# Sums of weight blocks on GpSimd in place of VectorE, in a fused encoder layer

## The chip, the cores and the metric

The kernel runs on one core of a Trainium2 chip. The metric is the device time of one execution in microseconds, taken as the median of several runs. A profile of one execution gives the rows that are read below. In it PE is the matrix engine TensorE (PEld its weight loads), DVE is VectorE, ACT is ScalarE, POOL is GpSimd and SP is SyncE, which issues most DMA transfers.

## What is computed

One layer of an encoder on 256 tokens of width 2048, in float32. After an attention half with two groups of heads comes a feed-forward half, and the change lies in that one:

```python
def conv_ffn(h, w_up_l, conv_w_l, conv_b_l, w_down_l):
    u = h @ w_up_l                       # 2048 -> 2 x 5632
    u = causal_depthwise_conv(u, width=3) + conv_b_l
    gate, val = jnp.split(u, 2, axis=-1)
    return (jax.nn.silu(gate) * val) @ w_down_l    # 5632 -> 2048

x = x + hybrid_mixer(rms_norm(x), ...)
x = x + conv_ffn(rms_norm(x), w_up, conv_w, conv_b, w_down)
```

## The kernel before

**Split weights.** Each float32 factor of a matmul is split in two parts, a rounded high part and the rest, and a product takes three matmuls: high by high, high by low and low by high. A block of weights is 128 partitions by 2048 numbers (1 MB). `load` (L201) issues its transfer on SP's queue into one of four raw buffers (`w_raw`). `split` makes the two parts: ScalarE rounds the block into `w_hi` (L208), then VectorE subtracts that from the raw block into `w_lo` (L209). There are three buffers for each part.

**The feed-forward half** is a list of steps. An up piece multiplies half of the depth for two blocks of 128 up-projection columns: 16 wide matmuls with the high part (L714) and 16 half-wide ones with the low part (L719), alternating two by two. After every second piece its result is evicted, on VectorE and ScalarE: L628 and L630 join the two halves of the accumulator and scale by the token factor, L637 and L644 form the convolution's terms, L649 adds them, and L655, L664, L667 and L669 form the gated product and its split.

**Products of blocks.** The hidden width is taken in parts: one of 4 blocks, then five of 8. While the up pieces of one part run, the down projection of the part before is done. For a part of 8 blocks this is `down_in_seven`, twice, for each half of the output columns. It multiplies 2 x 2 blocks of activations by 2 x 2 blocks of weights in seven products rather than eight, which needs sums of weight blocks. `w11`, `w12`, `w21` and `w22` are blocks of weights (1 MB each), and "w" is a buffer `w_sum`, of which there is one:

- product 1 uses "11", product 2 uses "21";
- product 3 uses "w" = "11" + "12" (the first sum);
- product 4 uses "w" = "w" + "22" (the second sum, in place);
- product 5 uses "12" + w22, product 6 uses "22", and product 7 uses "w" + w21. The additions for products 5 and 7 are made by transfers that accumulate into the block while they load it, issued from GpSimd's queue (L760).

There are four such parts, so 16 sums and 16 accumulating transfers. A product is 12 matmuls (L229) into a bank called `bank_a`, `bank_b` or `bank_c`; L733 then adds it to the tokens `x`. Activations need sums of their own (L678 to L691), once in a part.

**The order** of TensorE, VectorE, ScalarE and SP is written out by hand. At each step of the list the loop emits the loads of the step six ahead, the split of the step two ahead, the sums of the step four ahead, the matmuls of the step itself, and pieces of work that follow earlier steps:

```python
LOAD, SUM, SPLIT = 6, 4, 2
...
at(LOAD, 0)
follow()
at(SPLIT, 2)
follow()
at(SUM, 1)
at(0, 3)
```

Within a part, products alternate with up pieces, so that two steps lie between a product and the next. GpSimd is not in the hand-written order: the framework puts its instructions in order, and they wait for what they read and overwrite. All engines run their queues in order.

## Time and profile before

| | before |
|---|---|
| median of 3 runs | 1131.57 us (1130.93 to 1132.05) |
| span of the profiled execution, first to last instruction | 1129.0 us |
| TensorE busy | 1114.8 us, 99% of the span |
| VectorE busy | 843.3 us, 75% |
| ScalarE busy | 680.6 us, 60% |
| GpSimd busy | 20.9 us, 2% |
| HBM | 225.14 MB read, 201 GB/s over the span |

The profiled execution is told by its span; the median of the runs is 2.6 us longer. Rows of groups read: line, engine, operation, output<-input, shapes, count, then busy time in us and mean ns of one, then the idle time of that engine just before, with what ended it. Rows of the timeline read: start, duration, engine, line, operation, and in brackets idle time before it. Consecutive VectorE operations overlap a little in these rows: one of 2.28 us is followed by the next after 2.20. Rows of the chain read: start, length, what.

### The profile page before, as it was taken

The numbers are of one execution on the slowest core, as the hardware profiler recorded it, in microseconds if no ns is written. First come the engines' busy times: TensorE is split into PE (matmuls) and PEld (weight loads), VectorE is DVE, ScalarE is ACT, GpSimd is POOL, SyncE is SP. The second block draws the span as 40 slices with busy tenths as digits, with TensorE's granted clock in tenths as the row PEclk, the third lists the DMA queues.
The fourth block names the chain that finished last, engine by engine and source line by source line (L and its number), as shares of the span: only waits on it lengthen the run. The fifth ranks groups of instructions, "written<-read, shape, count | busy, mean of one in ns | idle before, by whom it ended". The sixth has DMA issues, their size and how long they took to land.

```text
span 1129.0 us, 14661 instructions
## 1 busy us (share of the span) xinstructions
PE 1114.8 (99%) x5890; PEld 956.6 (85%) x5890; DVE 843.3 (75%) x873; ACT 680.6 (60%) x840; POOL 20.9 (2%) x20
## 2 busy tenths in 40 slices
PE   7999999999999999999999999999999999999998
PEld 6998888888888888888888888888888888888886
DVE  4646656646556666766699898989989798989983
ACT  5644444445664566666667667766776667766751
POOL 0000000000000000000000000000000000000000
PEclk9999999999999999999999999999999999999999
DMA  7766555555444486555649697687949797696951
GB/s 234 219 206 218 171 158 159 185 159 178 149 149 150 149 256 199 188 190 192 195 144 252 220 268 249 187 265 195 290 149 242 240 252 242 188 288 182 291 172 66
DMA packets 170989, 228.17 MB, mean 202 GB/s; under 512 B 3992, under 2 KB 117802, under 8 KB 170922
## 3 DMA queue, kind: packets, MB, share of 16 engines
q1 hardware_dynamic: 162474, 210.47, 57.7%
q0 software_dynamic: 8448, 16.78, 8.6%
q8 instruction: 46, 0.75, 0.3%
q14 instruction: 21, 0.17, 0.0%
HBM read 225.14 MB, written 2.10 MB: 201 GB/s over the span
## 4 chain that ended last, share of the span: by engine, by line
PE 97%; DVE 1%; DMA 1%; ACT 0%; issue 0%; SPq 0%; DVEq 0%; ACTq 0%
PE pu L714 29%; PE acc L229 26%; PE pu L719 15%; PE bank_a L229 10%; PE pu L261 5%; PE bank_b L229 4%; PE pu L266 3%; PE bank_c L229 1%; DVE w_lo L209 1%; PE ps_x L148 1%; DMA x<-in_x_dram 0%; DMA w_raw<-in_w_up_dram 0%; PE ps_h L301 0%; ACT w_hi L208 0%; PE ps_z L511 0%
## 5 line engine op out<-in xcount | busy, mean ns | idle before, releaser
L209 DVE TENSOR_TENSOR w_lo<-w_raw,w_hi 128x2048 fp32r<-128x2048 f32 (+2 forms) x204 | 449.6, 2206 | 196.7 <-ACT w_hi L208 193.4
L208 ACT CAST w_hi<-w_raw 128x2048 fp32r<-128x2048 f32 (+2 forms) x204 | 376.0, 1843 | 248.5 <-PE acc L229 79.6
L714 PE MATMUL pu<-hT,w_hi 128*128 128x512 f32 x1408 | 441.7, 395 | 0.0
L719 PEld LDWEIGHTS pu<-hT,w_lo 128*128 128x128 f32 x1408 | 263.8, 188 | 65.8 <-DVE w_lo L209 4.6
L719 PE MATMUL pu<-hT,w_lo 128*128 128x256 f32 x1408 | 277.6, 278 | 0.9 <-DVE w_lo L209 0.9
L714 PEld LDWEIGHTS pu<-hT,w_hi 128*128 128x128 f32 x1408 | 218.8, 189 | 4.7
L229 PE MATMUL acc<-w_hi,hT 128*128 128x512 f32 (+1 forms) x640 | 143.3, 374 | 0.0
L229 PEld LDWEIGHTS acc<-w_hi,hT 128*128 128x128 f32 x640 | 114.2, 190 | 16.8
L261 PE MATMUL pu<-hT,w_hi 128*128 128x512 f32 x256 | 81.4, 399 | 0.0
L644 ACT ACTIVATE tap<-up,ccol 128x256 f32<-128x256 f32 x176 | 74.6, 495 | 0.0
L229 PE MATMUL acc<-w_lo,hT 128*128 128x512 f32 (+1 forms) x320 | 74.3, 371 | 0.0
L229 PEld LDWEIGHTS acc<-w_lo,hT 128*128 128x128 f32 x320 | 57.8, 189 | 8.7
L209 DVE TENSOR_TENSOR w_lo<-w_sum,w_hi 128x2048 fp32r<-128x2048 f32 x24 | 54.9, 2287 | 12.9 <-ACT w_hi L208 12.9
L208 ACT CAST w_hi<-w_sum 128x2048 fp32r<-128x2048 f32 x24 | 45.8, 1909 | 22.4 <-PE pu L714 20.0
L266 PEld LDWEIGHTS pu<-hT,w_lo 128*128 128x128 f32 x256 | 48.1, 188 | 11.4
L266 PE MATMUL pu<-hT,w_lo 128*128 128x256 f32 x256 | 50.4, 278 | 0.0
L229 PE MATMUL bank_a<-w_hi,g 128*128 128x512 f32 x192 | 47.0, 390 | 0.0
L229 PE MATMUL acc<-w_hi,oT 128*128 128x512 f32 x192 | 46.3, 393 | 0.0
L229 PEld LDWEIGHTS acc<-w_hi,oT 128*128 128x128 f32 x192 | 35.4, 188 | 7.0
L229 PEld LDWEIGHTS bank_a<-w_hi,g 128*128 128x128 f32 x192 | 34.5, 188 | 6.1
L261 PEld LDWEIGHTS pu<-hT,w_hi 128*128 128x128 f32 x256 | 39.0, 189 | 0.0
L637 ACT ACTIVATE gate<-up,ccol 128x256 f32<-128x256 f32 x44 | 24.0, 593 | 18.4 <-DVE up L630 18.4
(177 smaller groups left out, 1098.8 us busy)
## 6 DMA issues: line engine op xcount, KB each, us to landing
w_raw<-in_w_up_dram SPq DMA_DIRECT2D x88, 1024.0 KB, 9.9
w_raw<-in_w_down_dram SPq DMA_DIRECT2D x44, 1024.0 KB, 5.2
w_raw<-in_w_in_dram SPq DMA_DIRECT2D x36, 1024.0 KB, 5.3
w_raw<-in_w_out_dram SPq DMA_DIRECT2D x16, 1024.0 KB, 5.3
w_raw<-in_w_in_dram SPq DMA_DIRECT2D x12, 688.0 KB, 4.9
w_raw<-in_w_down_dram POOLq DMA_DIRECT2D x8, 1024.0 KB, 12.4
w_sum<-in_w_down_dram POOLq DMA_DIRECT2D x8, 1024.0 KB, 9.0
w_raw<-in_w_in_dram SPq DMA_DIRECT2D x8, 512.0 KB, 6.3
```

The source lines that it names most:

```text
L148: nc.tensor.transpose(ps[:, j, t * P : (t + 1) * P], xt[t][:, (k + j) * P : (k + j + 1) * P], ident)
L208: act.copy(hi[:, :n], raw[:, :n])
L209: dve.tensor_tensor(lo[:, :n], raw[:, :n], f32(hi[:, :n]), op=ALU.subtract)
L229: nc.tensor.matmul(o, lhs(i, l, t), r[:, i, :], start=starts and j == 0, stop=stops and j == 3 * n - 1, skip_group_check=len(accs) == 1 an ...
L261: nc.tensor.matmul(acc[:, j, :], hi[:, i, j * P : (j + 1) * P], hT[:, k].rearrange("p a b -> p (a b)"), start=k == 0, stop=False,)
L266: nc.tensor.matmul(acc[:, j, S:], lo[:, i, j * P : (j + 1) * P], hT[:, k, 0, :], start=False, stop=k == KT - 1,)
L637: act.activation(a[:, j, :], u[:, j, 2:], AF.Identity, scale=ccol[:, 2, f : f + 1], bias=ccol[:, 3, f : f + 1],)
L644: act.activation(taps[w][:, j, :], u[:, j, w : w + S], AF.Copy, scale=ccol[:, w, f : f + 1])
L714: nc.tensor.matmul(acc[:, j, :], hi[:, i, j * P : (j + 1) * P], hT[:, k].rearrange("p a b -> p (a b)"), start=k == 0, stop=False,)
L719: nc.tensor.matmul(acc[:, j, S:], lo[:, i, j * P : (j + 1) * P], hT[:, k, 0, :], start=False, stop=k == KT - 1,)
```

## The change

The two sums in each half of a part are issued on GpSimd rather than VectorE. Operands, buffers and shapes stay as they are.

```diff
             def sums():
                 if into not in mem:
                     mem[into] = wsum.tile([P, 2048], F32, name="w_sum", tag="w_sum")
-                dve.tensor_tensor(mem[into], mem[a], mem[b], op=ALU.add)
+                nc.gpsimd.tensor_tensor(mem[into], mem[a], mem[b], op=ALU.add)
 
             return sums
```

In the instruction lists, VectorE has 16 fewer rows, all L781. GpSimd has those 16 and one setup row ahead of them; its order is sum, accumulating transfer, sum, accumulating transfer, and so on. TensorE, ScalarE and SP have the same rows in the same order.

## The prediction

> **What bounds the kernel now.** I read the page first: its span, the busy time of each engine, and the chain that ended last.

> ```profile
> span 1129.0 us, 14661 instructions
> ...
> PE 1114.8 (99%) x5890; PEld 956.6 (85%) x5890; DVE 843.3 (75%) x873; ACT 680.6 (60%) x840; POOL 20.9 (2%) x20
> ...
> PE 97%; DVE 1%; DMA 1%; ACT 0%; issue 0%; SPq 0%; DVEq 0%; ACTq 0%
> ```

> The span is 1129.0 us and TensorE (PE) carries 97% of the chain, so the time is TensorE's own work. VectorE (DVE) is busy 75% of the span, but the sums run only in the FFN stage, so I asked the windows for that stage (columns: length, then busy time and instruction count of PE, weight load, DVE, ACT, POOL).

> ```profile
> 721.00:785.00 64.00, 63.79 (x336) 54.12 (x336) 57.69 (x47) 44.34 (x49) 3.73 (x3) 1.00 0.83 240
> ```

> Here VectorE works 57.69 of 64 us, and still TensorE lacks only 0.21 us. What TensorE lost to VectorE over the four parts that contain sums is in the waits (us in total, times, longest).

> ```profile
> PEld pu L719 <- DVE w_lo L209: 3.9, 8, 0.6
> ...
> PE pu L719 <- DVE w_lo L209: 0.6, 3, 0.2
> ```

> So VectorE is nearly full but almost never late. How much that costs is read from the chain. Each part runs 14 products (2.73 us) with an up piece between each two, and an undisturbed distance from product to product is 779.99 - 771.70 = 8.29 us.

> ```profile
> 712.92 2.73 PE bank_a L229 x12
> ...
> 729.99 2.75 PE bank_b L229 x12
> ...
> 738.52 2.73 PE bank_a L229 x12
> ...
> 771.70 2.73 PE bank_a L229 x12
> ...
> 779.99 2.73 PE bank_c L229 x12
> ...
> 796.58 2.73 PE bank_a L229 x12
> ```

> From the first product at 712.92 to the third at 729.99 it is 17.07 where two distances are 16.58, and to the fourth 8.53: 0.49 + 0.24 = 0.73 us lost in this part. The four parts with sums, which are built alike, lose about 4 x 0.73 = 2.9 us. That is all the change can win by making VectorE lighter. The profiled execution has a span of 1129.0, which is 2.6 below the median of 1131.57; the differences below are worked out inside that execution and laid on the median. About 0.2%, 2.3 us, is what a measurement of this kernel can tell from no change.

> **What moves.** The 16 sums leave VectorE's queue, four to a part.

> ```profile
> L781 DVE TENSOR_TENSOR w_sum<-w_sum,w_raw 128x2048 f32<-128x2048 f32 x8 | 18.3, 2288 | 0.3 <-DMA w_raw<-in_w_down_dram 0.2
> L781 DVE TENSOR_TENSOR w_sum<-w_raw 128x2048 f32<-128x2048 f32 x8 | 18.3, 2283 | 0.0
> ```

> That is 36.6 us of VectorE work, 2.20 each as a place in the queue (720.27 - 718.07 below). Nothing else changes place on VectorE, ScalarE, TensorE or SP. GpSimd's queue gets one setup row ahead of its first sum, which waits for nothing and stands in front of all of them, in a queue that is idle until the FFN stage: nothing; then, for each half of a part: sum, accumulating transfer into block "12", second sum, accumulating transfer into the sum. Both transfers' issues stood behind VectorE before, one after the first sum, the other after the low part of the second sum was split off.

> ```profile
> 720.88 1.28 POOL L760 DMA_DIRECT2D w_raw<-in_w_down_dram  x1 [54.24 <-DVE w_sum L781]
> 737.70 1.28 POOL L760 DMA_DIRECT2D w_sum<-in_w_down_dram  x1 [15.54 <-DVE w_lo L209]
> ```

> Now the first stands behind GpSimd's own sum, and the second sum stands behind the 1.28 us of the first issue. The second transfer (issued at 737.70) still waits for VectorE's split of the second sum and not for its own engine; its block is used only by the seventh product. These moves are free as long as a sum lasts under about 6 us (second rival).

> **How long a sum takes on GpSimd (T).** No row of before shows GpSimd arithmetic. The nearest from below is the same operation on VectorE, 2.28 us. From above there is the other way in which this queue adds one block onto another, the accumulating transfer, 9.0 us to landing.

> ```profile
> w_raw<-in_w_down_dram SPq DMA_DIRECT2D x44, 1024.0 KB, 5.2
> ...
> w_sum<-in_w_down_dram POOLq DMA_DIRECT2D x8, 1024.0 KB, 9.0
> ```

> The middle of the two in ratio is the square root of 2.28 x 9.0, 4.5; twice the VectorE row, which is the row nearest in kind, is 4.57. I take T = 4.57, and 3.4 to 6 as its likely range. [...]

> **Whether VectorE works beside it.** Between nothing and all of T: no row decides. The only overlap in the trace is an issue (720.88) beside the additions of L649 (720.27, 1.48 for two), which keep their length; an issue streams no block, so it says little. A sum streams three blocks of 2048 elements a partition from and to the memory that VectorE's own two-operand additions use at that moment. I hold it likelier than not that the two exclude each other, and take the upper end: a VectorE operation with both operands in SBUF stands still while GpSimd sums; one that reads an accumulator in PSUM (L628, L733) goes on. [...]

> **The price, sum by sum**, in one part. VectorE's rows around the first two sums, and the up piece's low-half matmul that waits for the split L209 behind each:

> ```profile
> 718.07 2.29 DVE L781 TENSOR_TENSOR w_sum<-w_raw 128x2048 f32<-128x2048 f32 x1
> 720.27 1.48 DVE L649 TENSOR_TENSOR gate<-gate,tap 128x512 f32<-128x512 f32 x2
> ...
> 722.27 2.28 DVE L209 TENSOR_TENSOR w_lo<-w_raw,w_hi 128x2048 fp32r<-128x2048 f32 x1
> ...
> 726.67 0.68 DVE L628 TENSOR_TENSOR t<-pu,t 128x512 f32<-128x512 f32 x1
> ...
> 728.00 2.28 DVE L781 TENSOR_TENSOR w_sum<-w_sum,w_raw 128x2048 f32<-128x2048 f32 x1
> ...
> 730.80 2.28 DVE L209 TENSOR_TENSOR w_lo<-w_raw,w_hi 128x2048 fp32r<-128x2048 f32 x1
> ```

> ```profile
> 724.61 0.50 PE L719 MATMUL pu<-hT,w_lo 128*128 128x256 f32 x2 [0.21 <-DVE w_lo L209]
> ```

> First sum. The load that it lacks is issued at 712.24 and takes 5.2, so its data are there at 717.4; VectorE runs a two-operand split until 718.07, and GpSimd starts then, exactly where the sum stood. VectorE's next operation, L649, has two SBUF operands and stands for T instead of 2.20. The split at 722.27 already ends too late for the matmul at 724.61, so the whole 4.57 - 2.20 = **2.37 us** is TensorE's.

> Second sum. It can start once the low part of the first sum is split off (726.67). L628 reads PSUM and runs beside it (0.72); L630 stands. VectorE loses 4.57 - 0.72 and saves 2.20: 1.65 late, and the split at 730.80 was late already by the 0.24 of the chain. **1.65 us**.

> ```profile
> 775.70 0.68 DVE L628 TENSOR_TENSOR t<-pu,t 128x512 f32<-128x512 f32 x1
> 776.42 0.69 DVE L630 TENSOR_TENSOR up<-t,R 128x512 f32<-128x512 f32 x1
> 777.03 2.28 DVE L781 TENSOR_TENSOR w_sum<-w_raw 128x2048 f32<-128x2048 f32 x1
> ...
> 779.83 2.28 DVE L209 TENSOR_TENSOR w_lo<-w_raw,w_hi 128x2048 fp32r<-128x2048 f32 x1
> ...
> 785.75 2.29 DVE L781 TENSOR_TENSOR w_sum<-w_sum,w_raw 128x2048 f32<-128x2048 f32 x1
> 787.96 0.68 DVE L733 TENSOR_TENSOR x<-x,bank_c 128x512 f32<-128x512 f32 x1
> 788.55 2.28 DVE L209 TENSOR_TENSOR w_lo<-w_raw,w_hi 128x2048 fp32r<-128x2048 f32 x1
> ```

> ```profile
> 783.01 0.40 PE L719 MATMUL pu<-hT,w_lo 128*128 128x256 f32 x2
> ```

> ```profile
> 791.30 0.40 PE L719 MATMUL pu<-hT,w_lo 128*128 128x256 f32 x2
> ```

> ```profile
> 712.24 0.37 SPq L201 DMA_DIRECT2D w_raw<-in_w_down_dram  x1
> ...
> 771.03 0.37 SPq L201 DMA_DIRECT2D w_raw<-in_w_down_dram  x1
> ...
> 779.34 0.37 SPq L201 DMA_DIRECT2D w_raw<-in_w_down_dram  x1
> ```

> Third sum. Its load (771.03) lands at 776.2, in the middle of L628. GpSimd sums from 776.2 to 780.8, and L630, due at 776.42, loses 4.35 and saves 2.20: 2.15 late. The split at 779.83 ends at 782.11, and TensorE asks for it at 783.01: 0.90 of slack. 2.15 - 0.90 = **1.25 us**.

> Fourth sum. Its block is loaded into the buffer that the third sum frees: in before the load went out at 779.34, when the sum ended, and landed by 785.75, 6.4 later. Now it lands at 780.8 + 6.4 = 787.2; VectorE comes to this place, 2.15 late, at 787.9, and the sum starts there. L733 (0.59, taken as 0.60) runs beside it, the split due at 788.55 stands: 4.57 - 0.60 - 2.20 = 1.77 more, 3.92 late in all. The slack of this split is 791.30 - (788.55 + 2.28) = 0.47, and TensorE is already 1.25 late: 3.92 - 0.47 - 1.25 = **2.20 us**.

> Sum of a part: 2.37 + 1.65 + 1.25 + 2.20 = 7.47; four parts: 29.9 us. Nothing gives it back: TensorE has no idle time, and VectorE's idle time later in a part only lets it catch up. As a formula a part costs 4T - 10.81. **Forecast: 1131.6 + 29.9 = 1161.5 us**, and for T from 3.4 to 6, 4 x 2.79 = 11.2 to 4 x 13.19 = 52.8: 1143 to 1184.

> **The rivals.**

> *They run side by side (faster).* VectorE is lighter by 2.20 ahead of the tight splits at 722.27 and 730.80, and the 0.73 a part goes: 1131.6 - 2.9 = 1128.7, at most. For it: the unchanged L649 beside the issue. Against: that issue streams nothing. It decides only while T stays under about 6, by the next rival's chain.

> *The sum itself comes late.* GpSimd yields to VectorE and takes its turns in the gaps, or is as slow as the transfer: T = 9 and VectorE unhurt. Then first sum 717.4 + 9.0 = 726.4; the load into the freed buffer lands 6.4 later, 732.8; second sum until 741.8; ScalarE's rounding of it (1.90, at 730.72 before) until 743.7, while TensorE starts the fourth product at 738.52: 5.2 late, eight times: 41.6 us, 1173 us.

> ```profile
> 730.72 1.90 ACT L208 CAST w_hi<-w_sum 128x2048 fp32r<-128x2048 f32 x1
> ```

> The point from which this chain decides is 717.4 + 2T + 6.4 + 1.9 = 738.5, T = 6.4 (about 6 in the second half: 776.2 + 2T + 8.3 = 796.58 gives 6.0). For it: GpSimd has no compute row to its name, and VectorE leaves it a tenth of the stage. Against: half the price of a transfer is enough to be in time.

> *They share evenly.* VectorE runs at half speed beside a sum: it loses T/2 = 2.29 and saves 2.20, 0.1 a sum, some 1.4 us over 16: 1133, no change.

> **How the numbers follow.** Exclusion, the forecast: 0.52. Side by side: 0.22. Late sums: 0.16. Even sharing: 0.10. Faster by over 0.2% needs nearly the whole 2.9 of the side-by-side case: 0.17; the rest of that case and half of the sharing are within 0.2%: 0.10; slower by over 0.2% is 0.73. The likeliest case's own range is 1143 to 1184. The stated range starts at 1128 to take in the side-by-side case, and ends at 1184, the exclusion case at T = 6; left out is a T beyond 6, about 0.15 in all.

> **What would show each step.** Right: 16 L781 rows on POOL of 4 to 6 us; a VectorE operation with two SBUF operands beside each that ends only when it ends, while L628 and L733 keep 0.68; waits of TensorE's low-half matmuls for w_lo of 1 to 3 us each, four to a part, some 30 us in all; TensorE's matmul rows otherwise as long as before. Wrong: VectorE rows of 2.28 and 1.48 unchanged beside a POOL sum and no TensorE wait in the stage (side by side); waits of bank_a matmuls for w_hi, with ScalarE behind a late sum (late sums); L781 rows on POOL much shorter or longer than 4.6, which moves the time by 16 us for each us of T; or the third and fourth sums free, if VectorE's idle time at 774 to 800 is worth more than the 0.90 and 0.47 read here.

## The result and the profile after

| | before | after |
|---|---|---|
| median of four runs | 1131.47 us (1130.93 to 1132.05) | 1165.01 us (1164.11 to 1167.08) |
| ratio to before, 95% interval | | 1.0299 (1.0284 to 1.0313) |
| span of the profiled execution | 1129.0 us | 1163.2 us |

The change makes the kernel 33.5 us slower; the prediction was 29.9 us, 1161.5 us. From the page after, the span, the busy time of the engines, and the chain by engine:

```profile
span 1163.2 us, 14680 instructions
...
PE 1124.0 (97%) x5890; PEld 961.8 (83%) x5890; DVE 875.0 (75%) x857; ACT 680.3 (58%) x840; POOL 97.2 (8%) x36
...
PE 76%; DVE 15%; issue 5%; ACT 3%; DMA 1%; SPq 0%; DVEq 0%; ACTq 0%
```

VectorE has lost 36.6 us of sums and is busy longer, 875.0 us where it was 843.3. Its share of the chain is 15% where it was 1%, and TensorE's is 76% where it was 97%. What TensorE waited for in the feed-forward stage, in the waits (us in total, times, longest):

```profile
PEld pu L719 <- DVE w_lo L209: 32.1, 16, 3.0
...
PE pu L719 <- DVE w_lo L209: 25.2, 14, 2.6
```

Before, these were 3.9 and 0.6. ScalarE, too, waited for sums (20.6 us in five waits), but TensorE waited for no product. The sums on GpSimd, by the view of the tile `w_sum` (duration in ns: least, median, greatest; first and last start):

```profile
L781 POOL TENSOR_TENSOR w_sum<-w_raw x8: 4597/4830/5627, 589.2 to 1062.4; 128x2048 f32<-128x2048 f32 x8
L781 POOL TENSOR_TENSOR w_sum<-w_sum,w_raw x8: 4585/4592/4615, 600.4 to 1074.5; 128x2048 f32<-128x2048 f32 x8
```

The second sums take 4.59 us; the prediction had taken 4.57. The rows of the first sums are longer, 4.81 to 5.63 us in five of the eight against 4.60 or 4.61 in the others, where the row begins while VectorE is still at work on operands in SBUF, so a row of GpSimd holds its wait as well. The timeline of VectorE around the four sums of one part, one of its rows on its own, and then GpSimd's:

```profile
736.78 0.68 DVE L628 TENSOR_TENSOR t<-pu,t 128x512 f32<-128x512 f32 x1
737.50 5.12 DVE L630 TENSOR_TENSOR up<-t,R 128x512 f32<-128x512 f32 x1
...
788.77 5.17 DVE L630 TENSOR_TENSOR up<-t,R 128x512 f32<-128x512 f32 x1
...
800.71 0.68 DVE L733 TENSOR_TENSOR x<-x,bank_c 128x512 f32<-128x512 f32 x1
801.31 6.32 DVE L209 TENSOR_TENSOR w_lo<-w_raw,w_hi 128x2048 fp32r<-128x2048 f32 x1
```

```profile
726.94 4.92 DVE L649 TENSOR_TENSOR gate<-gate,tap 128x512 f32<-128x512 f32 x1
```

```profile
725.68 5.63 POOL L781 TENSOR_TENSOR w_sum<-w_raw 128x2048 f32<-128x2048 f32 x1 [52.20 <-DMA w_raw<-in_w_down_dram]
...
737.48 4.58 POOL L781 TENSOR_TENSOR w_sum<-w_sum,w_raw 128x2048 f32<-128x2048 f32 x1 [4.58 <-DVE t L628]
...
788.77 4.61 POOL L781 TENSOR_TENSOR w_sum<-w_raw 128x2048 f32<-128x2048 f32 x1 [37.43 <-DVE t L628]
...
800.89 4.59 POOL L781 TENSOR_TENSOR w_sum<-w_sum,w_raw 128x2048 f32<-128x2048 f32 x1 [5.91 <-DVE w_lo L209]
```

Each sum has its VectorE operation that stands beside it. L649 at 726.94, one addition of 0.69, takes 4.92; L630 at 737.50 and at 788.77 takes 5.12 and 5.17 in place of 0.69; the split L209 at 801.31 takes 6.32 in place of 2.28. The three short ones end 0.56 us behind GpSimd's row, and the split 2.15 us behind it: each does its own work only when GpSimd has done. Of the operations that read PSUM, L733 at 800.71 keeps 0.68 with the sum's row beside it from 800.89 on, and that row its 4.59. L628 at 736.78 is over when the sum's row begins; at 1010.94, with a sum beside it from 1011.12 on, it takes 0.69. The first sum differs in a detail: its row begins at 725.68, the first of the two additions of L649 still goes ahead of it, and the second stands.

How late each sum makes TensorE is read from the first low-half matmul of the next up piece: it starts 0.46 us behind the first high-half one when nothing is late (1009.68 - 1009.22). The fourth part, one sum after the other:

```profile
1005.82 0.61 PE L714 MATMUL pu<-hT,w_hi 128*128 128x512 f32 x2
1008.88 0.50 PE L719 MATMUL pu<-hT,w_lo 128*128 128x256 f32 x2 [2.44 <-DVE w_lo L209]
1009.22 0.63 PE L714 MATMUL pu<-hT,w_hi 128*128 128x512 f32 x2
1009.68 0.40 PE L719 MATMUL pu<-hT,w_lo 128*128 128x256 f32 x2
```

```profile
1016.84 0.61 PE L714 MATMUL pu<-hT,w_hi 128*128 128x512 f32 x2
1019.14 0.50 PE L719 MATMUL pu<-hT,w_lo 128*128 128x256 f32 x2 [1.68 <-DVE w_lo L209]
```

```profile
1068.57 0.61 PE L714 MATMUL pu<-hT,w_hi 128*128 128x512 f32 x2
1070.38 0.51 PE L719 MATMUL pu<-hT,w_lo 128*128 128x256 f32 x2 [1.20 <-DVE w_lo L209]
```

```profile
1078.34 0.61 PE L714 MATMUL pu<-hT,w_hi 128*128 128x512 f32 x2
1081.28 0.51 PE L719 MATMUL pu<-hT,w_lo 128*128 128x256 f32 x2 [2.33 <-DVE w_lo L209]
```

The distances of 3.06, 2.30, 1.81 and 2.94 are 2.60, 1.84, 1.35 and 2.48 us too long, 8.27 in all. The same sum in before is 0.38 + 0.12 = 0.50, so this part grew by 7.8 us, where 7.47 was predicted. Over the four parts the distances grew by 26.2 us.

The other 8.5 us are new: in five places TensorE ran at half its clock after such a stall. The windows of 2 us after the first sum of the second part (the number behind POOL's is the granted clock), and the matmuls in and behind that stretch:

```profile
734.00:736.00 2.00, 1.29 (x6) 1.16 (x7) 2.00 (x2) 2.00 (x3) 0.00 (x0) 0.82 0.96 315
736.00:738.00 2.00, 2.00 (x8) 1.71 (x8) 1.97 (x3) 0.60 (x1) 0.52 (x1) 0.50 0.99 179
738.00:740.00 2.00, 2.00 (x12) 1.73 (x11) 2.00 (x1) 0.00 (x0) 2.00 (x1) 0.83 1.12 216
```

```profile
736.12 1.05 PE L714 MATMUL pu<-hT,w_hi 128*128 128x512 f32 x2
...
737.40 1.05 PE L714 MATMUL pu<-hT,w_hi 128*128 128x512 f32 x2
...
739.39 0.63 PE L714 MATMUL pu<-hT,w_hi 128*128 128x512 f32 x2
...
740.09 0.62 PE L714 MATMUL pu<-hT,w_hi 128*128 128x512 f32 x2
```

Two matmuls and the next two lie 1.28 us apart at 736.12 and 737.40, and 0.70 at 739.39 and 740.09. The clock lost in these windows is 0.18 x 2 + 0.50 x 2 + 0.17 x 2 = 1.7 us, and the five stretches, each 3.4 us long at 0.50, make 8.5. 26.2 + 8.5 = 34.7, against a span that grew by 34.2.

### The profile page after: what moved, and what is told of

Its sections match the earlier page's. It is cut to its first block, busy times and chain, and to the rows that moved or that the text cites. A ratio compares the mean times of both kernels' runs of the same rounds, so it can differ in the third digit from the quotient of the medians.

```text
span 1163.2 us, 14680 instructions
## 1 busy us (share of the span) xinstructions
PE 1124.0 (97%) x5890; PEld 961.8 (83%) x5890; DVE 875.0 (75%) x857; ACT 680.3 (58%) x840; POOL 97.2 (8%) x36
## 4 chain that ended last, share of the span: by engine, by line
PE 76%; DVE 15%; issue 5%; ACT 3%; DMA 1%; SPq 0%; DVEq 0%; ACTq 0%
PE acc L229 25%; PE pu L714 20%; PE pu L719 10%; DVE w_lo L209 9%; PE bank_a L229 8%; PE pu L261 5%; PE pu L266 3%; ACT w_hi L208 2%; PE bank_b L229 2%; DVE gate L649 1%; DVE up L630 1%; DVE x L733 1%; DVE t L628 1%; PE ps_x L148 1%; DVE s L691 1%
## 5 line engine op out<-in xcount | busy, mean ns | idle before, releaser
L209 DVE TENSOR_TENSOR w_lo<-w_raw,w_hi 128x2048 fp32r<-128x2048 f32 (+2 forms) x204 | 469.8, 2305 | 198.4 <-ACT w_hi L208 195.1
L208 ACT CAST w_hi<-w_raw 128x2048 fp32r<-128x2048 f32 (+2 forms) x204 | 376.0, 1843 | 243.7 <-PE acc L229 79.6
L714 PE MATMUL pu<-hT,w_hi 128*128 128x512 f32 x1408 | 447.0, 399 | 0.0
L719 PEld LDWEIGHTS pu<-hT,w_lo 128*128 128x128 f32 x1408 | 267.1, 191 | 94.6 <-DVE w_lo L209 32.8
L719 PE MATMUL pu<-hT,w_lo 128*128 128x256 f32 x1408 | 281.8, 282 | 25.6 <-DVE w_lo L209 25.4
L714 PEld LDWEIGHTS pu<-hT,w_hi 128*128 128x128 f32 x1408 | 221.8, 191 | 4.7
L229 PE MATMUL acc<-w_hi,hT 128*128 128x512 f32 (+1 forms) x640 | 142.8, 373 | 0.0
L229 PEld LDWEIGHTS acc<-w_hi,hT 128*128 128x128 f32 x640 | 114.1, 189 | 16.7
L781 POOL TENSOR_TENSOR w_sum<-w_raw 128x2048 f32<-128x2048 f32 x8 | 39.3, 4917 | 893.6 <-DMA w_raw<-in_w_down_dram 856.1
L261 PE MATMUL pu<-hT,w_hi 128*128 128x512 f32 x256 | 81.4, 399 | 0.0
L229 PE MATMUL acc<-w_lo,hT 128*128 128x512 f32 (+1 forms) x320 | 74.0, 370 | 0.0
L208 ACT CAST w_hi<-w_sum 128x2048 fp32r<-128x2048 f32 x24 | 45.6, 1899 | 34.5 <-POOL w_sum L781 20.6
L209 DVE TENSOR_TENSOR w_lo<-w_sum,w_hi 128x2048 fp32r<-128x2048 f32 x24 | 54.9, 2287 | 14.2 <-ACT w_hi L208 14.2
L229 PEld LDWEIGHTS acc<-w_lo,hT 128*128 128x128 f32 x320 | 57.4, 188 | 8.5
L630 DVE TENSOR_TENSOR up<-t,R 128x512 f32<-128x512 f32 x44 | 59.9, 1362 | 1.5
L266 PEld LDWEIGHTS pu<-hT,w_lo 128*128 128x128 f32 x256 | 48.1, 188 | 11.3
L266 PE MATMUL pu<-hT,w_lo 128*128 128x256 f32 x256 | 50.4, 278 | 0.0
L649 DVE TENSOR_TENSOR gate<-gate,tap 128x512 f32<-128x512 f32 x44 | 47.8, 1087 | 2.3
L229 PE MATMUL bank_a<-w_hi,g 128*128 128x512 f32 x192 | 47.0, 390 | 0.0
L229 PE MATMUL acc<-w_hi,oT 128*128 128x512 f32 x192 | 46.3, 393 | 0.0
L637 ACT ACTIVATE val<-up,ccol 128x256 f32<-128x256 f32 x44 | 24.1, 595 | 36.7 <-DVE up L630 36.6
## 6 DMA issues: line engine op xcount, KB each, us to landing
w_raw<-in_w_up_dram SPq DMA_DIRECT2D x88, 1024.0 KB, 9.2
w_raw<-in_w_down_dram SPq DMA_DIRECT2D x44, 1024.0 KB, 5.2
w_raw<-in_w_in_dram SPq DMA_DIRECT2D x36, 1024.0 KB, 5.3
w_raw<-in_w_out_dram SPq DMA_DIRECT2D x16, 1024.0 KB, 5.3
w_raw<-in_w_down_dram POOLq DMA_DIRECT2D x8, 1024.0 KB, 12.0
w_sum<-in_w_down_dram POOLq DMA_DIRECT2D x8, 1024.0 KB, 9.0
```

Of the source, the lines that this page charges most:

```text
L208: act.copy(hi[:, :n], raw[:, :n])
L209: dve.tensor_tensor(lo[:, :n], raw[:, :n], f32(hi[:, :n]), op=ALU.subtract)
L229: nc.tensor.matmul(o, lhs(i, l, t), r[:, i, :], start=starts and j == 0, stop=stops and j == 3 * n - 1, skip_group_check=len(accs) == 1 an ...
L261: nc.tensor.matmul(acc[:, j, :], hi[:, i, j * P : (j + 1) * P], hT[:, k].rearrange("p a b -> p (a b)"), start=k == 0, stop=False,)
L266: nc.tensor.matmul(acc[:, j, S:], lo[:, i, j * P : (j + 1) * P], hT[:, k, 0, :], start=False, stop=k == KT - 1,)
L630: dve.tensor_tensor(u[:, :, 2:], t2, R, op=ALU.mult)
```

## The experiments

The theory is the prediction's: while GpSimd sums, a VectorE operation with two operands in SBUF stands. The rival is that a sum on GpSimd is finished later, and that this lateness is what costs. Each run stands beside runs of the kernel before on the same chip.

| run | what it changes against before | median us | ratio to before (95%) | difference us |
|---|---|---|---|---|
| e1_beside_two | sums on VectorE, GpSimd adds beside | 1175.99 | 1.0384 (1.0365 to 1.0403) | +44.4 |
| e2_beside_copy | the same, GpSimd copies | 1142.60 | 1.0103 (1.0087 to 1.0120) | +11.0 |
| e3_beside_write | the same, GpSimd writes | 1131.70 | 1.0001 (0.9992 to 1.0010) | +0.1 |
| e4_first_only | first sums on GpSimd | 1150.76 | 1.0176 (1.0147 to 1.0205) | +19.0 |
| e5_second_only | second sums on GpSimd | 1144.56 | 1.0121 (1.0101 to 1.0140) | +13.0 |
| e6_half | half of each sum on GpSimd | 1143.75 | 1.0107 (1.0090 to 1.0124) | +12.0 |
| e7_quarters | each sum on GpSimd in four | 1183.61 | 1.0463 (1.0446 to 1.0481) | +51.8 |
| e8_short_sums | VectorE sums 64 columns only | 1129.27 | 0.9980 (0.9971 to 0.9989) | -2.3 |

**GpSimd beside sums that are not late (e1).** VectorE's sums stay, and GpSimd adds to a scratch tile.

```diff
                 dve.tensor_tensor(mem[into], mem[a], mem[b], op=ALU.add)
+                for i in range(4):
+                    part_b = mem[b][:, 512 * i : 512 * (i + 1)]
+                    nc.gpsimd.tensor_tensor(scr, part_b, part_b, op=ALU.add)
```

> VectorE makes its 16 sums as before; at each place GpSimd also adds the block of that sum to itself, four additions of 128x512 into a scratch tile that nothing reads. So no sum is later and only the company differs. Exclusion: VectorE operations with two SBUF operands stand for about 1.15 us at each of the 64 additions, some 74 us of standing with nothing saved; VectorE has about 12 us of idle time in a part of 128 us and catches part of it up, so 40 to 70 us slower than before, VectorE rows stretched beside POOL rows. Late sums (the rival: what costs is that GpSimd finishes a sum later): nothing waits for these additions, so within 3 us of before and VectorE rows of unchanged length.

It is 44.4 us slower though nothing reads what GpSimd adds. Two of VectorE's rows beside the additions:

```profile
734.27 3.12 DVE L209 TENSOR_TENSOR w_lo<-w_sum,w_hi 128x2048 fp32r<-128x2048 f32 x1
...
738.76 4.36 DVE L782 TENSOR_TENSOR w_sum<-w_sum,w_raw 128x2048 f32<-128x2048 f32 x1
```

A split of 2.28 takes 3.12 and a sum of 2.28 takes 4.36. Lateness of what GpSimd adds cannot do this, so the company of the two engines costs by itself. One thing besides the company did change: the accumulating transfers stand behind the additions in GpSimd's queue. But in this stage TensorE waits for nothing but VectorE's `w_lo`, and ScalarE never for a block of the down projection. The amount lies in the range of 40 to 70 for a reason that the range left out: measured as above, the distances grew by 31.9 us, and most of the rest is TensorE's clock (0.986 over the span, 0.999 in before).

**Copies and writes (e2, e3).** The same places, with `nc.gpsimd.tensor_copy(scr, part_b)` in e2, and in e3 a copy of one column and then eight times `nc.gpsimd.memset(scr, 0.0)`.

> The same with copies (one operand read) in place of additions. Exclusion by GpSimd's reads, whatever their number: a copy of 128x512 should take about half an addition, 0.6 us, 2.3 us at a place; with nothing saved that is about 2.3 + 1.6 + 1.2 + 1.6 = 6.7 us a part, 27 us slower. If only a second operand brings the two engines into each other's way: no change. Late sums: no change.

> The same with work that only writes: at each place a copy of one column, which fixes the time, and eight memsets of 128x512 into the scratch tile. If it is GpSimd's reading that stops VectorE: no change, within 3 us, and VectorE rows beside POOL rows keep 2.28 and 0.69 us. If any use of SBUF by GpSimd stops it: slower, by the length of the memsets, 15 us or more. Late sums: no change.

The copies cost 11.0 us. So one operand read by GpSimd is enough to stop VectorE; the amount was over-estimated. From VectorE's timeline in e2:

```profile
727.26 2.69 DVE L209 TENSOR_TENSOR w_lo<-w_sum,w_hi 128x2048 fp32r<-128x2048 f32 x1
...
731.20 3.03 DVE L782 TENSOR_TENSOR w_sum<-w_sum,w_raw 128x2048 f32<-128x2048 f32 x1
```

The split at 727.26 is 0.4 us longer than its 2.28, the sum at 731.20 0.75. A copy of 512 columns seems to hold VectorE up for about 0.4 us, not 0.6, and VectorE gets in between two copies. The writes cost nothing (+0.1 us). VectorE's timeline in e3, and rows of GpSimd's in the same stretch:

```profile
717.14 2.29 DVE L782 TENSOR_TENSOR w_sum<-w_raw 128x2048 f32<-128x2048 f32 x1
719.34 1.49 DVE L650 TENSOR_TENSOR gate<-gate,tap 128x512 f32<-128x512 f32 x2
...
721.35 2.29 DVE L209 TENSOR_TENSOR w_lo<-w_raw,w_hi 128x2048 fp32r<-128x2048 f32 x1
...
727.08 2.29 DVE L782 TENSOR_TENSOR w_sum<-w_sum,w_raw 128x2048 f32<-128x2048 f32 x1
```

```profile
716.86 3.21 POOL L783 COPY scr<-w_raw 128x1 f32<-128x1 f32 x1 [50.85 <-DMA w_raw<-in_w_down_dram]
720.14 3.45 POOL L785 MEMSET scr<- 128x512 f32 x6
...
726.38 4.62 POOL L785 MEMSET scr<- 128x512 f32 x8
```

Eight memsets take 4.62 us, as long as a sum, and VectorE's additions, split and second sum beside memsets keep 1.49, 2.29 and 2.29. Since the copies of e2 read and write and these only write, it is GpSimd's reading that stops VectorE.

**One sum of two (e4, e5).** For e4, and with the engines exchanged for e5:

```diff
-                dve.tensor_tensor(mem[into], mem[a], mem[b], op=ALU.add)
+                eng = nc.gpsimd if a == "11" else dve
+                eng.tensor_tensor(mem[into], mem[a], mem[b], op=ALU.add)
```

> Only the first sum of each half goes to GpSimd. Exclusion: 2.37 us for the first, 1.25 us for the third, and 0.43 us at the fourth's place (2.15 late less 1.25 and 0.47), 4.05 x 4 = 16.2 us, and 1.7 us more for each half-clock stretch of TensorE, which can follow the four stalls of about 2.4 us: 16 to 23 us. With the run that moves only the second sums it should add up to about the 33.5 us of the whole change. Late sums: little, 0 to 5 us.

> Only the second sum of each half goes to GpSimd, the first is VectorE's as before. Exclusion: by the prediction's steps the second sum costs 1.65 us and the fourth 1.77 - 0.47 = 1.30 us a part, together 2.95 x 4 = 11.8 us. Half-clock stretches of TensorE come after stalls of over 2 us; here none is that long, so the granted clock stays at 1.00 to the end of the last part. Late sums: the second sums are those that are followed most closely by a product, so they bring nearly all of the 33.5 us.

19.0 and 13.0 us, both as the exclusion says (16 to 23, and 11.8), and 31.9 together for the 33.5 of the whole change: the price goes by place, as in the prediction. In the profiled execution of e5 the longest stall was 2.1 us and the granted clock stayed at 1.00 through all four parts; in that of e4, with four stalls of 2.2 to 2.8 us, there was one stretch at half clock, after the longest. This differs from one execution to the next: another of e5 has a mean clock of 0.996 where the profiled one has 0.999, and is 3.5 us longer, and those of e4 go from 0.998 at 1148.8 us to 0.994 at 1156.3.

**Half a sum (e6).**

```diff
-                dve.tensor_tensor(mem[into], mem[a], mem[b], op=ALU.add)
+                for eng, s in ((nc.gpsimd, slice(0, 1024)), (dve, slice(1024, 2048))):
+                    eng.tensor_tensor(mem[into][:, s], mem[a][:, s], mem[b][:, s], op=ALU.add)
```

> Each sum is halved: GpSimd adds columns 0 to 1023, VectorE columns 1024 to 2047. Exclusion: VectorE stands 2.3 us for GpSimd's half and takes 1.1 for its own, 3.4 in place of 2.2; by the formula of the prediction with 3.4 for T that is 2.79 x 4 = 11 us slower, with no stall of over 2 us and the clock at 1.00. Late sums: a sum of two halves is ready sooner than before, so 0 to 3 us faster.

12.0 us slower, where the formula with 3.4 gave 11. VectorE's half of the first sum in one part:

```profile
720.24 3.42 DVE L782 TENSOR_TENSOR w_sum<-w_raw 128x1024 f32<-128x1024 f32 x1
```

VectorE stands for GpSimd's half and then does its own, 3.42 us in place of 2.29. So the sum is not ready sooner, as the expectation had it for the late sums, but about 1.1 us later; TensorE's waits in this stage are again for `w_lo` alone, and for no product.

**Four quarters (e7).**

```diff
-                dve.tensor_tensor(mem[into], mem[a], mem[b], op=ALU.add)
+                for i in range(4):
+                    s = slice(512 * i, 512 * (i + 1))
+                    nc.gpsimd.tensor_tensor(mem[into][:, s], mem[a][:, s], mem[b][:, s], op=ALU.add)
```

> All sums on GpSimd as in the changed kernel, each as four additions of 128x512. Exclusion with turns taken instruction by instruction: VectorE gets in between two quarters, so that no operation of it waits more than about 1.2 us at a time; the standing in all stays 4.6 to 5 us a sum, but the splits that TensorE waits for come sooner and the sum later: 10 to 33 us slower than before, at most as slow as the changed kernel. If GpSimd holds the way from its first quarter to its last: as the changed kernel, 33 us or slightly more. Late sums: as the changed kernel or later.

It is 51.8 us slower, well over the changed kernel. Both amounts given for exclusion missed; the "or later" of the late sums is what came. VectorE's timeline at the first sum of a part, GpSimd's second quarter in it, and the waits of the stage:

```profile
731.84 3.49 DVE L649 TENSOR_TENSOR gate<-gate,tap 128x512 f32<-128x512 f32 x2
...
735.85 2.78 DVE L209 TENSOR_TENSOR w_lo<-w_raw,w_hi 128x2048 fp32r<-128x2048 f32 x1
741.75 2.29 DVE L209 TENSOR_TENSOR w_lo<-w_sum,w_hi 128x2048 fp32r<-128x2048 f32 x1 [3.12 <-ACT w_hi L208]
```

```profile
733.04 1.73 POOL L783 TENSOR_TENSOR w_sum<-w_raw 128x512 f32<-128x512 f32 x1
```

```profile
ACT w_hi L208 <- POOL w_sum L783: 87.1, 16, 7.7
...
PE pu L719 <- DVE w_lo L209: 27.3, 18, 2.5
...
PE bank_a L229 <- ACT w_hi L208: 11.8, 8, 2.8
```

In this stretch the turns are taken one instruction at a time, as expected: the two additions of L649 take 3.49 in place of 1.48, and a quarter's row 1.73 us, its wait for VectorE included. But a sum now needs four turns, is ready only some 8 us after it began, and ScalarE waits 87.1 us for sums, so that VectorE in turn has no rounded block (3.12 us idle at 741.75) and TensorE waits for the product itself, 11.8 us, beside the 27.3 for the low parts of up pieces. That is the rival of late sums, which adds its part here and did not in the change; how the 51.8 us divide between late sums and standing was not measured. One long stop a sum is cheaper here than four turns.

**What there was to win (e8).** The sums are cut to 64 columns, on VectorE. They go into one tile that is set to zero at the start of the stage, so that the rest of it is defined.

```diff
-                dve.tensor_tensor(mem[into], mem[a], mem[b], op=ALU.add)
+                c = slice(0, 64)
+                dve.tensor_tensor(mem[into][:, c], mem[a][:, c], mem[b][:, c], op=ALU.add)
```

> VectorE sums only 64 of the 2048 columns at each of the 16 places (the rest of the sum is left out), and GpSimd adds nothing: this is what the change would have brought if the two engines ran side by side and every sum were in time. By the chain of the kernel before, 0.73 us a part, about 2.9 us faster, with no wait of TensorE for w_lo left in the four parts; if the chain overstates it, 1 to 2 us. That VectorE's 36.6 us of sums come off the time is excluded: TensorE had no idle time to give.

2.3 us faster, 0.2%. From the chain of this run, the first, third and fourth product of the same part as in the prediction:

```profile
712.13 2.73 PE bank_a L229 x12
...
728.71 2.73 PE bank_b L229 x12
...
737.01 2.73 PE bank_a L229 x12
```

16.58 and 8.30: the 0.73 is gone. With nearly all of the sums' 36 us off VectorE, no more than this comes off the time. No version among these that adds the whole blocks beats the kernel before.

## Why the prediction was right

- **What bounds the kernel** (TensorE, with VectorE nearly full and almost never late, and 2.9 us to win): held. The run without most of the sums won 2.3.
- **The length of a sum on GpSimd**, 4.57 between 2.28 and 9.0: 4.59 measured.
- **Exclusion**, which no row of before decided: shown, by the stretched rows beside each sum, by the PSUM readers that keep their length, and by e1 to e3; it was a choice at a chance of 0.52. Here GpSimd's reads stopped VectorE's two-operand instructions (+44.4 us in e1, +11.0 in e2), and its writes alone did not (+0.1 us in e3).
- **The price sum by sum**, as stalls with the 0.38 and 0.12 of before in them: 2.75, 1.77, 1.25 and 2.20 predicted, 2.60, 1.84, 1.35 and 2.48 measured in the part without a half-clock stretch. The chain's 0.49 and 0.24 of loss before read as 0.38 and 0.12 by this measure.
- **The total**: 29.9 predicted, 33.5 measured. The term that was missing is TensorE's clock, 8.5 us; the prediction's sign "matmul rows otherwise as long as before" did not hold. The term is larger than the difference because in the other parts a stretch at half clock delays TensorE and so hides part of the next stall: the second sum's is 0.26, 0.79 and 0.24 us in the first three parts and 1.84 in the fourth. So the stalls came to 26.2 in place of 29.9, against "nothing gives it back", and that the total is only 3.6 off is partly luck. The count of five belongs to the profiled execution: over the four, the mean granted clock goes from 0.989 to 0.995 and the time from 1164.1 to 1167.1.
- **Side by side**, priced at 1128.7 us: refuted as a description of the change, and right as the price of a sum that costs VectorE next to nothing (1129.3 in e8). **Even sharing**: refuted, since a stopped operation stands for the whole of GpSimd's.
- **Late sums**, with 41.6 us where a sum takes 9: not in the change, where no product waited for a sum, but e7, whose sums take about 8 us, lost 51.8 with 11.8 of it in just that wait.

## What to carry to other kernels

An engine that is 90% busy is not what a kernel waits for until something waits for it: 36.6 us of VectorE work were worth 2.3 us here, and that can be read beforehand from the chain, as the distance between steps against the undisturbed one. Before moving work from VectorE to GpSimd, ask whether GpSimd will read SBUF while VectorE runs instructions with two operands there. In this kernel that cost VectorE 3.8 to 4.5 us a sum, twice the 2.2 that it saved. Price such a move at the place where it stands, with the slack of the next thing that the critical engine asks for, and reckon that TensorE, once it stalls for about 2 us, can lose more than the stall: 8.5 us of clock beside 26.2 us of stalls here.

## What was not expected of the hardware

- **TensorE's clock halves after short stalls.** Five of the eight stalls between 2.2 and 2.8 us in the changed kernel were followed by about 3.4 us at a granted clock of 0.50, 1.7 us lost each time; three were not, one of 2.60 among them, nor were any of the shorter ones. In the profiled execution of e4 it was one of four, in that of e5 none. Which stalls do it can be read from the granted clock of the changed kernel: its half-clock stretches in the stage begin at 598.75, 670.43, 735.28, 871.82 and 943.50, which is 71.68, 64.85, 136.54 and 71.68 us apart, or 21, 19, 40 and 21 times 3.413. So they lie on one grid, and each stretch is about one step of it long. Two windows of that grid with a stall in them, and the window behind each (TensorE's busy time stands second, the granted clock behind POOL's numbers):

```profile
595.34:598.75 3.41, 1.14 (x6) 0.71 (x5) 3.41 (x4) 3.36 (x4) 0.42 (x1) 1.00 0.92 300
598.75:602.16 3.41, 3.41 (x12) 2.88 (x11) 3.38 (x3) 1.34 (x1) 1.71 (x1) 0.50 1.05 180
1004.94:1008.35 3.41, 1.50 (x7) 0.92 (x5) 3.31 (x4) 2.29 (x2) 1.30 (x1) 1.00 0.71 195
1008.35:1011.76 3.41, 2.88 (x16) 2.55 (x17) 3.38 (x4) 2.43 (x3) 0.64 (x1) 1.00 1.03 220
```
